# A depthwise convolution's taps, summed in a PSUM bank of their own and cut to the tokens that have an input

## The chip, the cores and the metric

One core of one Trainium2 chip runs the whole program. The metric is the device time of one execution in microseconds (us), lower is better. A kernel's time is the median of its runs.

## The reference, cut to what matters

Three blocks follow one another on 256 tokens of width 1024. The first is two layers of the code below, and the change is in its `_conformer_conv`; of the blocks behind (a recurrent part, an attention with compressed keys, MLPs) the change touches one accumulator only.

```python
for i in range(2):
    h = _rms_norm(x, norm_mix[i])
    q, k, v, cu, cg, ga, gb = split(h @ w_in[i])            # 512 each, ga and gb 1024
    y_a = _dilated_mixture_attention(rope(q), rope(k), v) @ w_attn_out[i]
    y_b = _conformer_conv(cu, cg, ...) @ w_conv_out[i] + b_conv_out[i]
    x = x + (sigmoid(ga) * y_a + sigmoid(gb) * y_b) @ w_out[i]
    x = x + _hier_moe(_rms_norm(x), ...)                    # 32 experts, then a gated projection
...
def _conformer_conv(cu, cg, w_dw, b_dw, ln_g, ln_b):        # 512 channels, 31 taps, causal
    u = cu * jax.nn.sigmoid(cg)
    y = lax.conv_general_dilated(u, rhs, window_strides=(1,), padding=[(CONV_K - 1, 0)], ...)
    return jax.nn.silu(_layer_norm(y + b_dw, ln_g, ln_b))
```

## The kernel before, in words

Activations lie transposed: 128 channels on the partitions, 256 tokens along them. A weight piece is loaded as fp32 (`wload`), cast to a high part on ScalarE (`whi`, L298), and the rest is taken on VectorE (`wlo`, L266); three passes of matmuls over the parts give one product. `ws` sums a strip of 256 output columns in one PSUM tile from the pool `acc` and then calls the strip's sink; `as_` sums two such tiles. `acc` has 4 of the 8 PSUM banks, `aux` the other 4.

A layer (`layer`) goes through: strips of w_in for the gate and the input of the convolution; then strips for q, k and v, with the rotary sinks on VectorE (L559, L560) and GpSimd (L562); attention by pairs of heads; eight strips for ga and gb; the norm of the convolution's result (`norm_silu`); four strips of w_attn_out, each with a sink on VectorE (`sink_a`, L639); four strips of w_conv_out, whose left operand is the normed convolution split in two (`split`, ACT L274 and DVE L275); and w_out. Behind it `moe_ple` streams the experts' weights.

The convolution is done on VectorE, for four groups of 128 channels: one TENSOR_SCALAR for the first tap (L504) and 30 SCALAR_TENSOR_TENSOR (L507), each of which multiplies 256 tokens of `u` (shifted by one) with a weight of each channel and adds what has been summed so far. `u` has 30 zeros in front, so that every tap has 256 tokens. The taps are a generator in the background (`self.bg`): every `wload` pulls four of them (`behind(BG)`), every pair of heads five, and ahead of `norm_silu` the rest is pulled.

`norm_silu` takes the mean over the channels by four matmuls with a matrix of ones (`pm`), subtracts it (L526), squares (ScalarE, L527), sums the squares by eight matmuls of one column each (`pcol`, 16 rows in the trace), forms the reciprocal root (DVE L346, GpSimd L347), spreads it over the tokens by a diagonal matrix (`dg`, L377) and two matmuls (four rows), then multiplies (L539), scales (L540), applies tanh (ScalarE, L542) and the product (L543), and splits (L274, L275).

The order of the instructions on each engine is made before the run: a scheduler takes the program's operations and places them by a simulated timeline (`schedule_with_timeline_sim=True`), under the pools' limits. Each engine then executes its own list strictly in order. SP issues the weight loads; big tiles for activations and for expert pieces come from one pool of slots named `mw`, so an expert piece can be fetched ahead only once a slot is free. In the trace every tile of that pool has the name mw: `u`, the sums, the gates and the expert pieces alike.

Of the kernel before, what the change touches and what calls it, by code (L numbers as in the profile page):

```python
# [16 lines left out]
ALU = mybir.AluOpType  # L17
AX = mybir.AxisListType
PSUM = bass.MemoryType.PSUM
# [3 lines left out]
T = 256  # L23
# [6 lines left out]
CK = 31  # L30
# [15 lines left out]
NACC = 4  # L46
# [172 lines left out]
class Kern:  # L219
    def __init__(self, ctx, tc, a, out):  # L220
        self.tc, self.nc, self.a, self.out, self.ctx = tc, tc.nc, a, out, ctx
        self.uid = 0
        self.bg = iter(())
        ec = ctx.enter_context
        self.cp = ec(tc.tile_pool(name="cp", bufs=1))
        self.wp = ec(tc.tile_pool(name="wp", bufs=WP))
        self.wq = ec(tc.tile_pool(name="wq", bufs=WQ))
        self.sm = ec(tc.tile_pool(name="sm", bufs=2))
        self.acc = ec(tc.tile_pool(name="acc", bufs=NACC, space=PSUM))
        self.aux = ec(tc.tile_pool(name="aux", bufs=8 - NACC, space=PSUM))  # L230
        self.hp = ec(tc.tile_pool(name="hp", bufs=3))
        self.loads, self.gates = [], ()
        self.dr = ec(tc.tile_pool(name="dr", bufs=1, space=DRAM))
# [3 lines left out]
        return f"{s}_{self.uid}"  # L237

    def ps(self, pool=None):
        return (pool or self.acc).tile([P, 512], F32, tag="ps", name=self.n("ps"))  # L240

    def h8(self, dt=F32):
# [41 lines left out]
    def wload(self, key, nk, p0=0):  # L284

        nc = self.nc
        raw = self.wp.tile([P, 1024], F32, tag="raw", name=self.n("raw"))
        o, kp, n = BL[key]
        ps = slice(p0, p0 + kp)
        self.loads.append(nc.sync.dma_start(raw[ps, :n], self.block(key)))  # L290
        if len(self.loads) in self.gates:
            with self.tc.issue_after(self.loads[-1].ins):
                i = len(self.ahead)
                self.ahead.append(self.epiece(self.mr, "mw", *self.first_piece(i)))
        hi = self.wq.tile([P, 1024], F32R, tag="whi", name=self.n("whi"))
        lo = self.wq.tile([P, 1024], F32R, tag="wlo", name=self.n("wlo"))
        hv, lv = hi[ps, :n], lo[ps, :n]
        nc.scalar.copy(hv, raw[ps, :n])  # L298
        self.sub(lv, raw[ps, :n], hv)
        self.behind(BG)  # L300
        r = "p (k n) -> p k n"
        return hv.rearrange(r, k=nk), lv.rearrange(r, k=nk)
# [155 lines left out]
    def layer(self, l):  # L458
        nc, tc, a = self.nc, self.tc, self.a
        vec = self.vec  # L460
        self.l = l
        w_in = ("w_in", l)
        act = self.act_h
        if l == 0:
# [9 lines left out]
        with tc.tile_pool(name=f"d1_{l}", bufs=1) as dp:  # L474

            s8 = self.slot
            r4 = lambda t, o=0: t[:, o:o + 4 * T].rearrange("p (c t) -> p c t", c=4)
            r8 = lambda t: t[:, :8 * T].rearrange("p (c t) -> p c t", c=8)
            u = s8()[:, :4 * (T + CK - 1)].rearrange("p (c t) -> p c t", c=4)
            nc.gpsimd.memset(u[:, :, :CK - 1], 0.0)  # L480

            dB = s8()
            thc = r4(dB)
            quarter = lambda i: dB[:, i * 512:(i + 1) * 512].rearrange("p (c t) -> p c t", c=2)
            vcs = s8()
            cacc = r4(vcs)
            v = vcs[:, 4 * T:8 * T].rearrange("p (t n) -> p t n", t=2)
            w0, bd = VEC["w_dw", l], VEC["b_dw", l]
# [7 lines left out]

            def sink_cu(c, ps):
                c = 2 * (c - 6)
                nc.vector.tensor_tensor(u[:, c:c + 2, CK - 1:], thc[:, c:c + 2, :], ps, op=ALU.mult)

            def conv(cs):
                for c in cs:
                    wc = w0 + c * CK
                    nc.vector.tensor_scalar(cacc[:, c, :], u[:, c, 0:T], vec[:, wc:wc + 1], vec[:, bd + c:bd + c + 1], op0=ALU.mult, op1=ALU.add)  # L504
                    yield
                    for j in range(1, CK):
                        nc.vector.scalar_tensor_tensor(cacc[:, c, :], u[:, c, j:j + T], vec[:, wc + j:wc + j + 1], cacc[:, c, :],  # L507
                                                       op0=ALU.mult, op1=ALU.add)
                        yield
            for i in range(2):  # L510
                self.ws(w_in, 2048 + 256 * i, 256, P, act, sink_cg)
                if l == 0 and i == 1:
                    with tc.issue_after(self.loads[5].ins):
                        nc.sync.dma_start(self.cst[:, 2 * P:], a["consts"][:, 2 * P:])
                        nc.sync.dma_start(self.rv, a["rv"])
                        nc.sync.dma_start(self.nv, a["nv"])
                self.ws(w_in, 1536 + 256 * i, 256, P, act, sink_cu)
                self.bg = itertools.chain(self.bg, conv((2 * i, 2 * i + 1)))
# [392 lines left out]

    def moe_ple(self, l):
        nc, tc, a = self.nc, self.tc, self.a
        self.npiece, self.gates, self.ny = 0, (), 0
        with tc.tile_pool(name=f"m1_{l}", bufs=1) as mp:
            posm, posr, gE, gates = self.route(l, mp)
            pp = self.slot().rearrange("p (t d) -> p t d", t=2)
# [180 lines left out]
    def block2(self):  # L1098
        nc, tc, a, cp = self.nc, self.tc, self.a, self.cp
        vec = self.vec  # L1100
# [18 lines left out]
        with tc.tile_pool(name="rn", bufs=1) as rp, tc.tile_pool(name="rn2", bufs=2) as r2:  # L1119
# [43 lines left out]
            for b in range(4):  # L1163
# [6 lines left out]
                for o in range(3):  # L1170
                    c = 3 * b + o
# [51 lines left out]
        with tc.tile_pool(name="ns1", bufs=1) as sp_, tc.tile_pool(name="ns2", bufs=2) as s2p, tc.tile_pool(name="ns3", bufs=4) as s3p:  # L1223
            s8 = lambda dt=F32: sp_.tile([P, 2080], dt, tag="s8", bufs=4, name=self.n("s8"))
# [41 lines left out]
            nc.gpsimd.memset(hid, 0.0)  # L1266
            w2 = sp_.tile([P, 2, 2, HD], F32, name="w2")
            hs_ = sp_.tile([P, 256], F32, name="hs")
            php = self.ps()
            nz = NG * NC_  # L1270
            phi = ("phi_k", "phi_v")
            for kv, nm in enumerate(phi):
# [19 lines left out]
            for i in range(2):  # L1292
# [9 lines left out]
                for c in range(4 * i, 4 * i + 4, 2):  # L1302
                    ps = self.ps(self.aux)
# [4 lines left out]
            for i in range(2):  # L1308
# [10 lines left out]
                ps = self.ps(self.aux)  # L1319
# [2 lines left out]
                        nc.tensor.transpose(ps[:, gp * T + tt * P:gp * T + (tt + 1) * P], kn[:, tt, gp * P:(gp + 1) * P], self.ident)  # L1322
                nc.scalar.activation(kT[:, 0:2, i, :], ps.rearrange("p (g t) -> p g t", g=2), AF.Copy, scale=nv[:, 1 + i:2 + i])

            pht = self.ps(self.aux)
            for kv in range(2):
                o = 64 * kv
# [15 lines left out]
            ps = self.ps(self.aux)  # L1343
# [12 lines left out]
            ps = self.ps(self.aux)  # L1356
# [4 lines left out]
            ps = self.ps(self.aux)  # L1361
# [10 lines left out]
            for cp_ in range(2):  # L1372
                ps = self.ps(self.aux)
# [5 lines left out]
            for tt in range(2):  # L1379
# [6 lines left out]
                pv = pc[:, tt, :, :, 0:ncb].rearrange("p r g c -> p (r g) c")  # L1386
# [13 lines left out]
            for r in range(4):  # L1400
                ps = self.ps(self.aux)
# [8 lines left out]
            for c in range(8):  # L1410
# [3 lines left out]
                for tt in range(2):  # L1414
                    w = P if tt == 0 else T
# [134 lines left out]
```

## Time and profile before

| | us |
|---|---|
| median of 3 runs | 1913.4 (1908.98 to 1913.78) |
| profiled execution | 1918.83, its span 1916.7 |
| layer 0 / layer 1 in the span | about 0 to 200 / 660 to 865 |
| expert stages | about 210 to 645, and to 1310 |
| last blocks | about 1320 to 1916 |
| busy over the span: TensorE, VectorE, ScalarE, GpSimd | 1634.9, 855.2, 577.8, 61.4 |
| granted TensorE clock, mean | 0.906 of full speed |

The shares of the whole span hide the stages: the two layers use all engines, the two expert stages wait for the memory. The layers, where the change is, have to be read by themselves.

### The profile page before, as it was taken

Reading aid. Unit: us, or ns where it says so; the run is one execution under the profiler, and the core shown is the slowest. Engines: PE = TensorE matmul, PEld = TensorE weight load, DVE = VectorE, ACT = ScalarE, POOL = GpSimd, SP = SyncE. Lnnn points to the kernel's source line nnn. Section 1 sums busy time; section 2 is a strip of 40 time slices with the busy share of each in tenths; the row PEclk is TensorE's granted clock in tenths of the full one; section 3 lists DMA queues with packets and bytes.
Section 4 is the critical chain, followed back from the end, with each engine's and each line's share of the span. In section 5 each row is a group of like instructions: output and inputs, shape, how many; then the busy total and the mean of one; then the engine's idle time right before and its main releaser. Section 6 shows DMA issues by size and latency. Waiting matters only on the chain. (4 is left out here: it accounts for less than half of the span.)

```text
span 1916.7 us, 28139 instructions
## 1 busy us (share of the span) xinstructions
PE 1634.9 (85%) x11355; PEld 1099.3 (57%) x11355; DVE 855.2 (45%) x1760; ACT 577.8 (30%) x1033; POOL 61.4 (3%) x74
## 2 busy tenths in 40 slices
PE   8998887766767999989766576689999999999999
PEld 8898431221213698884311221147897778679987
DVE  8987220111101399862110110015888656556643
ACT  4455110001001445541100000025464444445532
POOL 0100000000000010000000000000011100000000
PEclk9999897787788999999978887899999989789999
DMA  7658899999999675598999999995757633235554
GB/s 284 220 177 302 339 426 427 427 425 426 427 427 426 281 277 165 193 334 356 426 427 427 424 426 426 427 426 205 219 167 237 203 99 104 66 98 186 185 190 134
DMA packets 109725, 567.29 MB, mean 296 GB/s; under 512 B 12106, under 2 KB 21258, under 8 KB 61712
## 3 DMA queue, kind: packets, MB, share of 16 engines
q1 hardware_dynamic: 102976, 558.45, 75.3%
q10 hardware_dynamic: 5984, 5.82, 1.0%
q8 instruction: 94, 1.54, 0.3%
q0 software_dynamic: 624, 1.09, 0.2%
q14 instruction: 47, 0.39, 0.1%
HBM read 561.48 MB, written 3.83 MB: 295 GB/s over the span
## 5 line engine op out<-in xcount | busy, mean ns | idle before, releaser
L261 PE MATMUL ps<-mw,h 128*32 128x512 f32 x2032 | 319.5, 731 | 131.3 <-DMA mw<-in_w_exp_up_dram 70.6
L298 ACT CAST whi<-raw 128x1024 fp32r<-128x1024 f32 (+3 forms) x286 | 294.8, 1034 | 445.2 <-PE ps L261 222.9
L266 DVE TENSOR_TENSOR wlo<-raw,whi 128x1024 fp32r<-128x1024 f32 (+3 forms) x286 | 342.5, 1200 | 183.3 <-ACT whi L298 173.9
L261 PE MATMUL ps<-h,whi 128*128 128x256 f32 x2208 | 293.8, 282 | 4.9 <-ACT h L413 2.4
L261 PEld LDWEIGHTS ps<-h,whi 128*128 128x128 f32 x2208 | 273.3, 188 | 10.3 <-ACT h L413 3.4
L261 PEld LDWEIGHTS ps<-mw,h 128*32 128x32 f32 x2032 | 50.5, 118 | 338.2 <-DMA mw<-in_w_exp_up_dram 164.2
L261 PE MATMUL ps<-mw,mw 128*32 128x512 f32 (+3 forms) x1584 | 144.2, 466 | 39.9 <-DMA mw<-in_w_exp_down_dram 34.2
L261 PE MATMUL ps<-h,wlo 128*128 128x256 f32 x1104 | 154.4, 281 | 0.5 <-DVE wlo L266 0.5
L261 PEld LDWEIGHTS ps<-h,wlo 128*128 128x128 f32 x1104 | 140.4, 188 | 1.3 <-DVE wlo L266 0.7
L910 DVE TENSOR_TENSOR x<-x,ps 128x512 f32<-128x512 f32 (+2 forms) x60 | 34.6, 581 | 217.2 <-PE ps L261 217.2
L845 ACT ACTIVATE mw<-ps 128x512 f32<-128x512 f32 x16 | 9.5, 596 | 401.1 <-PE ps L261 401.1
L846 DVE TENSOR_TENSOR mw<-mw,ps 128x512 f32<-128x512 f32 x16 | 11.0, 687 | 266.7 <-issue 141.9
L261 PEld LDWEIGHTS ps<-mw,mw 128*32 128x32 f32 (+1 forms) x1584 | 47.3, 115 | 123.6 <-DMA mw<-in_w_exp_down_dram 69.2
L507 DVE SCALAR_TENSOR_TENSOR mw<-mw,vec,mw 128x256 f32<-128x256 f32 x240 | 111.3, 510 | 0.0
L261 PEld LDWEIGHTS ps<-h,h 128*128 128x128 f32 x512 | 68.0, 205 | 63.7 <-issue 55.2
L818 DVE TENSOR_TENSOR h<-ps,vec 128x256 f32<-128x256 f32 (+1 forms) x80 | 29.7, 371 | 167.3 <-PE ps L261 167.2
L261 PE MATMUL ps<-whi,h 128*128 128x512 f32 (+1 forms) x512 | 104.2, 345 | 0.0
L261 PE MATMUL ps<-mw 128*128 128x512 f32 (+4 forms) x328 | 91.1, 447 | 14.4 <-ACT mw L904 14.2
L261 PE MATMUL ps<-h,h 128*128 128x128 f32 x512 | 78.2, 299 | 16.0 <-issue 10.5
L261 PEld LDWEIGHTS ps<-whi,h 128*128 128x128 f32 x512 | 79.0, 190 | 16.3 <-issue 3.8
L261 PEld LDWEIGHTS ps<-mw 128*128 128x128 f32 (+1 forms) x328 | 45.4, 196 | 60.2 <-ACT mw L904 35.8
L904 ACT COPY mw<-ps 128x512 f32<-128x512 f32 (+2 forms) x50 | 21.6, 432 | 193.1 <-PE ps L261 193.1
(340 smaller groups left out, 1850.7 us busy)
## 6 DMA issues: line engine op xcount, KB each, us to landing
mw<-in_w_exp_gate_dram SPq DMA_DIRECT2D x128, 1024.0 KB, 19.6
mw<-in_w_exp_up_dram SPq DMA_DIRECT2D x126, 1024.0 KB, 19.6
mw<-in_w_exp_down_dram SPq DMA_DIRECT2D x118, 1024.0 KB, 19.6
raw<-in_w_in_dram SPq DMA_DIRECT2D x129, 512.0 KB, 4.5
raw<-in_w_mlp_in_dram SPq DMA_DIRECT2D x32, 512.0 KB, 3.5
raw<-in_w_mlp_out_dram SPq DMA_DIRECT2D x32, 512.0 KB, 3.5
raw<-in_w_out_dram SPq DMA_DIRECT2D x24, 512.0 KB, 4.4
raw<-in_w_ple_gate_dram SPq DMA_DIRECT2D x16, 512.0 KB, 16.8
```

Source lines behind the costliest of these rows:

```text
L261: return self.nc.tensor.matmul(out, lhsT, rhs, start=start, stop=stop)
L266: self.nc.vector.tensor_tensor(lo, src, hi.bitcast(F32), op=ALU.subtract)
L298: nc.scalar.copy(hv, raw[ps, :n])
L507: nc.vector.scalar_tensor_tensor(cacc[:, c, :], u[:, c, j:j + T], vec[:, wc + j:wc + j + 1], cacc[:, c, :], op0=ALU.mult, op1=ALU.add)
L818: nc.vector.tensor_tensor(xg[:, k:k + n, :], ps[:, :n * P].rearrange("p (k s) -> p k s", k=n), self.vec[:, gcol + k:gcol + k + n].unsqueez ...
L845: nc.scalar.activation(sg, G, AF.Silu)
L846: nc.vector.tensor_tensor(sg, sg, U, op=ALU.mult)
L904: nc.scalar.copy(ys[i], Y[:, :dw])
L910: nc.vector.tensor_tensor(xs, xs, pc[:, :dw], op=ALU.add)
```

## The change

The pool `acc` gets three banks, and a new pool `one` gets the fourth. Outside the layers every fourth accumulator comes from `one`, as if nothing had changed; inside a layer (`apart`) `one` belongs to the convolution and the strips go round on three. The convolution's running sum lies in a tile of `one`, two channel groups in one tile, and the last tap writes the result to SBUF. `u` loses its 30 zeros: tap d works on tokens d to 255 alone, 256 - d of them, in the order d = 0, 30, 29, ... 1; since the tap d = 1 writes tokens 1 to 255 only, a copy on ScalarE carries token 0 of each group over. One accumulator (`php`) of a later block also comes from `one`.

```diff
@@ -226,7 +226,10 @@
         self.wp = ec(tc.tile_pool(name="wp", bufs=WP))
         self.wq = ec(tc.tile_pool(name="wq", bufs=WQ))
         self.sm = ec(tc.tile_pool(name="sm", bufs=2))
-        self.acc = ec(tc.tile_pool(name="acc", bufs=NACC, space=PSUM))
+        self.acc = ec(tc.tile_pool(name="acc", bufs=NACC - 1, space=PSUM))
+
+        self.one = ec(tc.tile_pool(name="one", bufs=1, space=PSUM))
+        self.apart, self.nps = False, 0
         self.aux = ec(tc.tile_pool(name="aux", bufs=8 - NACC, space=PSUM))
         self.hp = ec(tc.tile_pool(name="hp", bufs=3))
         self.loads, self.gates = [], ()
@@ -237,6 +240,10 @@
         return f"{s}_{self.uid}"
 
     def ps(self, pool=None):
+        if pool is None and not self.apart:
+            self.nps += 1
+            if self.nps % NACC == 0:
+                pool = self.one
         return (pool or self.acc).tile([P, 512], F32, tag="ps", name=self.n("ps"))
 
     def h8(self, dt=F32):
@@ -458,7 +465,7 @@
     def layer(self, l):
         nc, tc, a = self.nc, self.tc, self.a
         vec = self.vec
-        self.l = l
+        self.l, self.apart = l, True
         w_in = ("w_in", l)
         act = self.act_h
         if l == 0:
@@ -476,13 +483,12 @@
             s8 = self.slot
             r4 = lambda t, o=0: t[:, o:o + 4 * T].rearrange("p (c t) -> p c t", c=4)
             r8 = lambda t: t[:, :8 * T].rearrange("p (c t) -> p c t", c=8)
-            u = s8()[:, :4 * (T + CK - 1)].rearrange("p (c t) -> p c t", c=4)
-            nc.gpsimd.memset(u[:, :, :CK - 1], 0.0)
+            u = r4(self.held())
 
             dB = s8()
             thc = r4(dB)
             quarter = lambda i: dB[:, i * 512:(i + 1) * 512].rearrange("p (c t) -> p c t", c=2)
-            vcs = s8()
+            vcs = self.held()
             cacc = r4(vcs)
             v = vcs[:, 4 * T:8 * T].rearrange("p (t n) -> p t n", t=2)
             w0, bd = VEC["w_dw", l], VEC["b_dw", l]
@@ -496,17 +502,21 @@
 
             def sink_cu(c, ps):
                 c = 2 * (c - 6)
-                nc.vector.tensor_tensor(u[:, c:c + 2, CK - 1:], thc[:, c:c + 2, :], ps, op=ALU.mult)
+                nc.vector.tensor_tensor(u[:, c:c + 2, :], thc[:, c:c + 2, :], ps, op=ALU.mult)
+
 
             def conv(cs):
+                pv = self.ps(self.one).rearrange("p (c t) -> p c t", c=2)
                 for c in cs:
-                    wc = w0 + c * CK
-                    nc.vector.tensor_scalar(cacc[:, c, :], u[:, c, 0:T], vec[:, wc:wc + 1], vec[:, bd + c:bd + c + 1], op0=ALU.mult, op1=ALU.add)
+                    w = lambda d: vec[:, w0 + c * CK + CK - 1 - d:w0 + c * CK + CK - d]
+                    ac = pv[:, c % 2]
+                    nc.vector.tensor_scalar(ac, u[:, c, :], w(0), vec[:, bd + c:bd + c + 1], op0=ALU.mult, op1=ALU.add)
                     yield
-                    for j in range(1, CK):
-                        nc.vector.scalar_tensor_tensor(cacc[:, c, :], u[:, c, j:j + T], vec[:, wc + j:wc + j + 1], cacc[:, c, :],
-                                                       op0=ALU.mult, op1=ALU.add)
+                    for d in range(CK - 1, 0, -1):
+                        dst = cacc[:, c, :] if d == 1 else ac
+                        nc.vector.scalar_tensor_tensor(dst[:, d:], u[:, c, :T - d], w(d), ac[:, d:], op0=ALU.mult, op1=ALU.add)
                         yield
+                    nc.scalar.copy(cacc[:, c, 0:1], ac[:, 0:1])
             for i in range(2):
                 self.ws(w_in, 2048 + 256 * i, 256, P, act, sink_cg)
                 if l == 0 and i == 1:
@@ -911,7 +921,7 @@
 
     def moe_ple(self, l):
         nc, tc, a = self.nc, self.tc, self.a
-        self.npiece, self.gates, self.ny = 0, (), 0
+        self.npiece, self.gates, self.ny, self.apart = 0, (), 0, False
         with tc.tile_pool(name=f"m1_{l}", bufs=1) as mp:
             posm, posr, gE, gates = self.route(l, mp)
             pp = self.slot().rearrange("p (t d) -> p t d", t=2)
@@ -1266,7 +1276,8 @@
             nc.gpsimd.memset(hid, 0.0)
             w2 = sp_.tile([P, 2, 2, HD], F32, name="w2")
             hs_ = sp_.tile([P, 256], F32, name="hs")
-            php = self.ps()
+            self.apart = True
+            php = self.ps(self.one)
             nz = NG * NC_
             phi = ("phi_k", "phi_v")
             for kv, nm in enumerate(phi):
@@ -1322,6 +1333,7 @@
                         nc.tensor.transpose(ps[:, gp * T + tt * P:gp * T + (tt + 1) * P], kn[:, tt, gp * P:(gp + 1) * P], self.ident)
                 nc.scalar.activation(kT[:, 0:2, i, :], ps.rearrange("p (g t) -> p g t", g=2), AF.Copy, scale=nv[:, 1 + i:2 + i])
 
+            self.apart = False
             pht = self.ps(self.aux)
             for kv in range(2):
                 o = 64 * kv
```

How the change moves instructions shows on two engines. First VectorE, layer 0, around the sinks of attn_out (L639 before, L649 now). `mw_844` and `mw_852` are the gate that a sink updates, `wlo` a weight's low part, `mw_168` before and `ps_832` now the running sum, L526 and L536 the first step of `norm_silu` behind the taps. Before:

```order
L626 TENSOR_TENSOR mw_846<-ps_1568,rB_154 128x512
L266 TENSOR_TENSOR wlo_1699<-raw_1696,whi_1698 128x1024
L507 SCALAR_TENSOR_TENSOR mw_168<-mw_165,vec,mw_168 128x256 x3
L275 TENSOR_TENSOR mw_841<-ps_1019,mw_841 128x256
L507 SCALAR_TENSOR_TENSOR mw_168<-mw_165,vec,mw_168 128x256 x5
L639 SCALAR_TENSOR_TENSOR mw_844<-mw_844,ps_1631 128x512
L266 TENSOR_TENSOR wlo_1731<-raw_1728,whi_1730 128x1024
L526 TENSOR_TENSOR mw_168<-mw_168,ps_1449 128x256 x4
L639 SCALAR_TENSOR_TENSOR mw_844<-mw_844,ps_1663 128x512
L266 TENSOR_TENSOR wlo_1763<-raw_1760,whi_1762 128x1024
L639 SCALAR_TENSOR_TENSOR mw_844<-mw_844,ps_1695 128x512
```

Now, the sinks of the third and the fourth strip and what follows (the widths go on from 239 to 251 between this piece and the next):

```order
L649 SCALAR_TENSOR_TENSOR mw_852<-mw_852,ps_1705 128x512
L517 SCALAR_TENSOR_TENSOR ps_832<-mw_168,vec,ps_832 128x234
L273 TENSOR_TENSOR wlo_1810<-raw_1807,whi_1809 128x1024
L517 SCALAR_TENSOR_TENSOR ps_832<-mw_168,vec,ps_832 128x235
L649 SCALAR_TENSOR_TENSOR mw_852<-mw_852,ps_1737 128x512
L517 SCALAR_TENSOR_TENSOR ps_832<-mw_168,vec,ps_832 128x236
L273 TENSOR_TENSOR wlo_1847<-raw_1844,whi_1846 128x1024
L517 SCALAR_TENSOR_TENSOR ps_832<-mw_168,vec,ps_832 128x237
L517 SCALAR_TENSOR_TENSOR ps_832<-mw_168,vec,ps_832 128x238
```
```order
L517 SCALAR_TENSOR_TENSOR ps_832<-mw_168,vec,ps_832 128x252
L517 SCALAR_TENSOR_TENSOR ps_832<-mw_168,vec,ps_832 128x253
L517 SCALAR_TENSOR_TENSOR ps_832<-mw_168,vec,ps_832 128x254
L517 SCALAR_TENSOR_TENSOR mw_171<-mw_168,vec,ps_832 128x255
L536 TENSOR_TENSOR mw_171<-mw_171,ps_1459 128x256 x4
```

Before, the last tap stands ahead of the first sink of attn_out. Now 20 taps of the last channel group (widths 236 to 255) stand behind the sink of the fourth strip; in layer 1 it is 18.

Second TensorE, the same place: strips of attn_out (`mw_841` or `mw_849` on the left), the matmuls of the norm (`ones`, `cst`, `dg`), and the first of conv_out (`mw_842` or `mw_850`). Before:

```order
L261 MATMUL ps_1727<-mw_841,whi_1730 128x256 x12
L261 MATMUL ps_1462<-cst,mw_167 128x1
L261 MATMUL ps_1727<-mw_841,whi_1730 128x256
L261 MATMUL ps_1462<-cst,mw_167 128x1
L261 MATMUL ps_1727<-mw_841,whi_1730 128x256 x3
L261 MATMUL ps_1727<-mw_841,wlo_1731 128x256 x6
L261 MATMUL ps_1462<-cst,mw_167 128x1
L261 MATMUL ps_1727<-mw_841,wlo_1731 128x256
L261 MATMUL ps_1462<-cst,mw_167 128x1 x5
L261 MATMUL ps_1727<-mw_841,wlo_1731 128x256
L261 MATMUL ps_1476<-dg_1475,cst 128x128 x2
L261 MATMUL ps_1759<-mw_842,whi_1762 128x256
```

Now:

```order
L268 MATMUL ps_1705<-mw_849,whi_1708 128x256 x16
L268 MATMUL ps_1705<-mw_849,wlo_1709 128x256 x8
L268 MATMUL ps_1737<-mw_849,whi_1740 128x256 x16
L268 MATMUL ps_1737<-mw_849,wlo_1741 128x256 x8
L268 MATMUL ps_1459<-mw_171,ones_92 128x256
L268 MATMUL ps_1472<-cst,mw_170 128x1 x8
L268 MATMUL ps_1486<-dg_1485,cst 128x128 x2
L268 MATMUL ps_1769<-mw_850,whi_1772 128x256
```

Before, the norm's matmuls are mixed into the strips of attn_out. Now they stand behind its last strip, and there is nothing else for TensorE between that strip and conv_out.

Further ahead a count is enough: on VectorE 39 taps stand ahead of the low part of the first piece of v's weights in layer 0 before and 25 now, in layer 1 41 before and 26 now.

## Rows read from the trace of the kernel before

**Rows 1.** The page: chain of work that ended last, by engine.
```profile
PE 27%; DVE 2%; DMA 1%; ACT 1%; issue 0%; DVEq 0%; ACTq 0%
```

**Rows 2.** Stretches: length, busy PE, PEld, DVE, ACT, POOL; clock, DMA share, GB/s.
```profile
48.00:96.00 48.00, 45.33 (x312) 39.92 (x312) 48.00 (x101) 22.59 (x42) 8.21 (x11) 0.96 0.62 219
...
150.00:160.00 10.00, 4.17 (x28) 3.81 (x28) 7.58 (x22) 3.40 (x9) 0.72 (x1) 0.74 0.80 251
200.00:210.00 10.00, 6.98 (x33) 4.16 (x32) 5.94 (x37) 2.32 (x7) 0.49 (x1) 0.52 0.45 174
300.00:400.00 100.00, 72.24 (x390) 16.94 (x388) 9.22 (x18) 4.12 (x7) 0.00 (x0) 0.76 1.01 427
```

**Rows 3.** Timeline of TensorE: start, duration, what; idle before and releaser.
```profile
65.53 1.58 PE L261 MATMUL ps<-wlo,h 128*128 128x512 f32 x4 [2.55 <-DVE wlo L266]
...
725.00 1.20 PE L261 MATMUL ps<-wlo,h 128*128 128x512 f32 x4 [0.99 <-DVE wlo L266]
...
729.24 1.20 PE L261 MATMUL ps<-wlo,h 128*128 128x512 f32 x4 [1.17 <-DVE wlo L266]
```

**Rows 4.** Timeline of TensorE, layer 0, end of attn_out to conv_out.
```profile
143.46 0.59 PE L261 MATMUL ps<-mw,ones 128*128 128x256 f32 x2
...
150.52 1.17 PE L261 MATMUL ps<-cst,mw 128*128 128x1 f32 x10
151.55 0.36 PE L261 MATMUL ps<-mw,wlo 128*128 128x256 f32 x1
154.12 0.68 PE L261 MATMUL ps<-dg,cst 128*128 128x128 f32 x4 [2.21 <-DVE dg L377]
158.43 5.38 PE L261 MATMUL ps<-mw,whi 128*128 128x256 f32 x31 [3.63 <-ACT mw L274]
```

**Rows 5.** Timeline of TensorE, layer 1, the same place.
```profile
811.15 0.60 PE L261 MATMUL ps<-dg,cst 128*128 128x128 f32 x4
816.65 5.45 PE L261 MATMUL ps<-mw,whi 128*128 128x256 f32 x31 [4.89 <-ACT mw L274]
```

**Rows 6.** Timeline of VectorE, layer 0: last taps, first sink, wlo, subtractions.
```profile
139.08 2.06 DVE L507 SCALAR_TENSOR_TENSOR mw<-mw,vec,mw 128x256 f32<-128x256 f32 x5
143.42 0.69 DVE L639 SCALAR_TENSOR_TENSOR mw<-mw,ps 128x512 f32<-128x512 f32 x1 [2.28 <-PE ps L261]
144.03 1.22 DVE L266 TENSOR_TENSOR wlo<-raw,whi 128x1024 fp32r<-128x1024 f32 x1
145.16 1.41 DVE L526 TENSOR_TENSOR mw<-mw,ps 128x256 f32<-128x256 f32 x4
```

**Rows 7.** Timeline of VectorE, layer 1: root, diagonal, first multiplication.
```profile
809.26 0.15 DVE L346 TENSOR_SCALAR ms<-ps 128x2 f32<-128x2 f32 x1
810.25 0.48 DVE L377 TENSOR_SCALAR dg<-cst,rc 128x128 f32<-128x128 f32 x2 [0.83 <-POOL rc L347]
...
813.09 1.41 DVE L539 TENSOR_TENSOR mw<-mw,ps 128x256 f32<-128x256 f32 x4
```

**Rows 8.** Groups by line and form: busy us, mean ns of one; idle before.
```profile
L507 DVE SCALAR_TENSOR_TENSOR mw<-mw,vec,mw 128x256 f32<-128x256 f32 x240 | 111.3, 510 | 0.0
L414 DVE SCALAR_TENSOR_TENSOR h<-ps,vec,h 128x256 fp32r<-128x256 f32 x32 | 14.2, 480 | 1.4 <-ACT h L413 0.8 <-PE ps L261 0.5
L910 DVE TENSOR_TENSOR x<-x,ps 128x256 f32<-128x256 f32 x12 | 5.1, 422 | 45.0 <-PE ps L261 44.9
L527 ACT ACTIVATE mw<-mw 128x256 f32<-128x256 f32 x8 | 2.9, 408 | 0.0
```

**Rows 9.** Line 507 by itself: min/median/max ns, first and last start.
```profile
L507 DVE SCALAR_TENSOR_TENSOR mw<-mw,vec,mw x240: 448/479/971, 29.1 to 798.5; 128x256 f32<-128x256 f32 x120
```

**Rows 10.** Timelines of VectorE and GpSimd, layer 0, rotary sinks.
```profile
53.84 2.22 DVE L507 SCALAR_TENSOR_TENSOR mw<-mw,vec,mw 128x256 f32<-128x256 f32 x3
...
52.87 1.65 POOL L562 TENSOR_TENSOR mw<-mw 128x256 f32<-128x256 f32 x1 [3.86 <-DVE mw L560]
```

**Rows 11.** Timeline of SyncE's queue: first expert piece issued behind the taps.
```profile
141.17 0.33 SPq L800 DMA_DIRECT2D mw<-in_w_exp_up_dram  x1
```

## The prediction

> **What bounds the kernel now.** I read the chain that ended last first: TensorE holds by far the largest share of it, 27%, VectorE 2% [rows 1]. So a change on VectorE counts only where TensorE waits for it. Next come the stretches. In the q and k strips of layer 0 VectorE is busy for all of 48 us, while TensorE works 45.33 of them [rows 2]: both are near full. Between attn_out and conv_out it is the other way: in the 10 us from 150 on TensorE is busy for 4.17, at a granted clock of 0.74. The expert stage behind the layer is bound by memory: 427 GB/s and DMA engines full from 300 to 400. But at 200 to 210, where it begins, they are busy for 0.45 only, so this stage begins when the layer lets it and a later layer moves it whole.
>
> Then the waits of TensorE in the layers. It waits for a weight's low part, which stands behind taps on VectorE, 2.55 us once in layer 0 and 0.99 and 1.17 us in layer 1 [rows 3]. And it waits for the norm of the convolution: attn_out's last matmul ends at 151.55 + 0.36 = 151.91, conv_out begins at 158.43 [rows 4]; in layer 1 the ends are 811.15 and 816.65 [rows 5]. The last taps of layer 0 end at 139.08 + 2.06 = 141.14, ahead of attn_out's first sink at 143.42 [rows 6]; so the mean, the squares and the sums run under attn_out, and only the last part of the norm is seen.
>
> **What a tap costs.** Five taps in a row take 2.06 us [rows 6]; with the median of 0.479 us for one [rows 9] they start (2.06 - 0.48) / 4 = 0.395 us apart. What a token costs: VectorE needs 422 ns for 256 columns with a PSUM operand [rows 8] and 0.69 us for 512 [rows 6], so (690 - 422) / 256 = 1.04 ns. The mean tap loses 15.5 tokens, 16 ns, and 120 taps of a layer 1.9 us. The taps of the tail, 237 to 255 tokens, lose 10 ns: 0.39 us each.
>
> What a tap costs with its sum in PSUM no row shows, since no VectorE row writes there. Reading is shown: the same operation with one input in PSUM and a scalar per partition takes 480 ns [rows 8], against the taps' median of 479; a plain sum with one PSUM input takes 422. I take no change, as the 480 row is the same operation. Below lies 422 (-0.06 us), above the taps that met GpSimd's rotary work: three in 2.22 us [rows 10], 0.74 each, +0.35. That upper row is two engines on SBUF, which a sum in PSUM should ease rather than add, so I hold the far end for unlikely.
>
> [...]
>
> **The change, part by part.** The order of the instructions decides, and it moves. (1) Fewer taps ahead of the first wlo of v: in layer 0 25 instead of 39 stand there, in layer 1 26 instead of 41; 14 x 0.395 = 5.5 us is more than the 2.55 us and the 0.99 + 1.17 us that TensorE waited [rows 3]. I let these waits go: -2.55 and -2.16 us.
>
> (2) The norm's matmuls leave the strips of attn_out. The 16 column matmuls cost 1.17 / 10 = 0.117 us each [rows 4], 1.87 us; one of the mean's goes too, and two of its rows stand 143.46 to 143.70, 0.24 us. With (1), attn_out ends at 151.91 - 2.55 - 1.87 - 0.24 = 147.25 in layer 0 and at 811.15 - 2.16 - 1.87 - 0.24 = 806.88 in layer 1. Three accumulators in place of four cost nothing by this: a sink takes 0.69 us on VectorE [rows 6], a strip has 24 matmuls between two sinks, and its bank is wanted again only two strips later.
>
> (3) The tail. Behind attn_out's last matmul VectorE does that strip's sink (0.6 us to the next start, 143.42 to 144.03), a tap (0.4), a wlo (1.13, 144.03 to 145.16 [rows 6]) and 19 taps at 0.39, 7.4 us; with 0.1 for the handover 9.6 us in layer 0, and with 17 taps 8.85 in layer 1. All of this was done before attn_out ended; now TensorE has nothing else to do and stands.
>
> (4) The chain behind the last tap, which in part was hidden and now is seen whole: ScalarE's copy of token 0, 0 to 0.41 us (the longer by the 408 ns of a whole row of 256 [rows 8]), I take 0.3; one mean matmul 0.59 [rows 4], four subtractions 1.41 [rows 6], the last square 0.41 [rows 8], the column matmuls 1.17 [rows 4] (ten of the sixteen rows, as before: those that stand behind the last square), from the root to the end of the diagonal's matmuls 809.26 to 811.15 + 0.60, 2.49 us [rows 5, 7], and from the first multiplication to conv_out 813.09 to 816.65, 3.56 us [rows 5, 7]. That is 9.93, and with 0.4 for handovers 10.3 us. TensorE comes to it from a pause; the clock in such a stretch was 0.74 in the mean [rows 2], and I add 1.17 us, the column matmuls at half speed (0 to 1.2).
>
> (5) Sum. Conv_out begins at 147.25 + 9.6 + 10.3 + 1.2 = 168.4 in place of 158.43, +10.0 us, and in layer 1 at 806.9 + 8.85 + 10.3 + 1.2 = 827.2 in place of 816.65, +10.6 us: together +20.6. Nothing behind takes it back: the expert stage starts with the layer, and the first expert piece behind the taps is issued at 141.17, right after the last tap freed its slot [rows 11], so fetching ahead starts some 15 us later too; that piece is not needed before 200. The accumulator of the later block I cost at nothing: a block with TensorE as its bound has it under matmuls, and a strip that had to wait for the bank's sink would lose the 0.69 us of one. The zeros of `u` that go and the clears that come lie on GpSimd, busy 8.21 of 48 us [rows 2]; without that cover they would cost a wait of under 1 us.
>
> The profiled execution took 1918.83 us, 5.4 more than the median of 1913.4; the sum gives 1939 for a profile and **1934 us** for the median.
>
> **The rivals.** A is the sum. Without the clock's 2.3 us, with taps of 0.06 us less (38 x 0.06 = 2.3) it is 1929; with TensorE's waits of (1) left as they are (+4.7) and taps 0.1 us dearer (+3.8), 1942.
>
> B: a tap with its sum in PSUM is much dearer. The tail pays at once, 3.8 us for each 0.1 us. The other 104 taps of a layer have cover: VectorE has 20 taps less to do ahead of attn_out's end, 8 us, and 1.9 us by the shorter ones, so 0.1 us on each is free; above it each 0.1 us delays attn_out by 10 us a layer, since VectorE is full there [rows 2]. At +0.2 us: 7.6 + 20.8 more than A, about 1962; at +0.13 about 1945. Against it stands the 480 row.
>
> C: the expert stage takes the delay up, because pieces fetched ahead cover its beginning; then 1913 to 1924, by how much of the 20.6 us is absorbed. For it speaks that the DMA engines are not full at 200 to 210, so that a burst could be caught up; against it that the slots are full by then and the stage itself runs at 427 GB/s, which leaves no room.
>
> D, faster: taps are relieved. Their mean is 510 against a median of 479 ns [rows 8, 9], and three beside GpSimd's work took 2.22 us [rows 10]; with one operand less in SBUF this goes, 240 x 31 ns = 7.4 us of VectorE, the waits of (1) go with it, and 1913.4 - 4.7 = 1909 would be left if the tail were hidden. It decides only if the tail and the norm's chain fit between 147.25 and 158.43, in 11.2 us. The chain alone takes 10.3, so the order would have to let the 20 taps run earlier, and it puts them behind the sink; D then needs TensorE to gain over 8 us a layer before attn_out, where it was idle for 2.67 us of 48 [rows 2].
>
> **How the numbers follow.** A 0.62, B 0.16, C 0.11, D 0.11. A alone spans 1929 to 1942. The range 1916 to 1952 leaves out D (0.11), half of C (0.05) and the end of B (0.04). What a measurement of this kernel can tell from no change is about 0.3%, 5.7 us. Faster: most of D and a little of C, 0.10. Same: the rest of D and a part of C, 0.08. Slower: 0.82.
>
> **What would show it.** Right: in layer 0 TensorE ends attn_out near 147, VectorE works through 20 taps at 0.39 us without a gap, conv_out starts near 168, and near 837 in layer 1; the waits before the first v strip are gone; the expert stages are as long as before. Wrong: taps in PSUM 0.1 us or more off 0.39; conv_out at 160 or before; expert stages shorter by what the layers lost.

## The result, and the profile after

The change made the kernel slower: 1937.43 us median of 6 runs (1924.74 to 1944.34) against 1910.77 of 6 (1906.62 to 1913.78), ratio 1.0133, 95% interval 1.0107 to 1.016. The forecast was 1934, and the layers behave as case A had it, but for the spacing of the taps. The profiled execution has a span of 1933.6 us.

The order put 20 taps behind attn_out's last sink; the timeline of VectorE in layer 0 of the changed kernel shows them (against [rows 6]):

```profile
145.27 0.46 DVE L517 SCALAR_TENSOR_TENSOR ps<-mw,vec,ps 128x236 f32<-128x236 f32 x1
145.64 1.22 DVE L273 TENSOR_TENSOR wlo<-raw,whi 128x1024 fp32r<-128x1024 f32 x1
146.78 9.20 DVE L517 SCALAR_TENSOR_TENSOR ps<-mw,vec,ps 128x237 f32<-128x237 f32 x18
156.02 0.48 DVE L517 SCALAR_TENSOR_TENSOR mw<-mw,vec,ps 128x255 f32<-128x255 f32 x1
158.00 1.42 DVE L536 TENSOR_TENSOR mw<-mw,ps 128x256 f32<-128x256 f32 x4 [1.50 <-PE ps L268]
```

The last tap ends at 156.50, before it was 141.14. Between the first of the eighteen and the last tap lie 156.02 - 146.78 = 9.24 us: 0.513 us a tap, not 0.39. Over the whole layer the widths in the trace run from 226 to 255 four times over, so one channel group is finished before the next begins. TensorE, the same place (against [rows 4]):

```profile
143.53 1.10 PE L268 MATMUL ps<-mw,wlo 128*128 128x256 f32 x8
156.74 1.22 PE L268 MATMUL ps<-mw,ones 128*128 128x256 f32 x2 [12.11 <-ACT mw L519]
158.98 3.58 PE L268 MATMUL ps<-cst,mw 128*128 128x1 f32 x16 [1.02 <-ACT mw L537]
163.93 1.22 PE L268 MATMUL ps<-dg,cst 128*128 128x128 f32 x4 [1.37 <-DVE dg L384]
168.91 5.32 PE L268 MATMUL ps<-mw,whi 128*128 128x256 f32 x31 [3.76 <-ACT mw L281]
```

Attn_out ends at 144.63, 7.3 us earlier than before, and then TensorE stands for 12.11 us and goes through the norm's chain alone: 24.3 us to conv_out, where there were 6.5. The wait is put down to ScalarE's copy of token 0 (L519), but the copy itself stood behind the last tap and took 0.16 us from 156.53. Layer 1, TensorE (against [rows 5]):

```profile
817.58 1.10 PE L268 MATMUL ps<-mw,wlo 128*128 128x256 f32 x8
829.79 1.22 PE L268 MATMUL ps<-mw,ones 128*128 128x256 f32 x2 [11.11 <-ACT mw L519]
...
841.89 3.35 PE L268 MATMUL ps<-mw,whi 128*128 128x256 f32 x14 [3.69 <-ACT mw L281]
```

The stretches of [rows 2], now:

```profile
150.00:160.00 10.00, 2.24 (x7) 1.52 (x7) 7.48 (x17) 1.52 (x5) 0.00 (x0) 0.50 0.32 108
...
48.00:96.00 48.00, 48.00 (x347) 42.58 (x347) 43.98 (x86) 26.05 (x49) 8.10 (x6) 1.00 0.62 209
300.00:400.00 100.00, 70.63 (x408) 18.68 (x412) 8.91 (x19) 3.54 (x6) 0.00 (x0) 0.80 1.01 427
```

From 150 to 160 TensorE works 2.24 us, at a granted clock of 0.50, after it stood for 12.11 us. In the q and k strips it is now busy for all 48 us and VectorE is relieved, 43.98: the change does give what a reader of the diff would hope for, but ahead of the place where it loses more. The expert stage is as it was, 427 GB/s from 300 to 400.

To see where the time goes, these are marks of the profiles: the first conv_out sink of layer 0 (a), the first gate sink of layer 1 (b), the first conv_out sink of layer 1 (c), the last sum of the second expert stage (d), and the rest of the span behind it (e). Each kernel has one profile, before and after have two (the second are runs r1 and r2 below).

| kernel | a | b | c | d | e |
|---|---|---|---|---|---|
| before | 166.1 | 681.6 | 824.4 | 1318.6 | 598.1 |
| before, again | 166.5 | 682.4 | 825.3 | 1322.1 | 586.0 |
| after | 176.5 | 693.9 | 850.7 | 1345.5 | 588.1 |
| after, again | 177.4 | 693.6 | 850.1 | 1345.2 | 593.8 |
| e1, sum in SBUF | 164.9 | 683.2 | 823.9 | 1320.4 | 595.3 |
| e2, two banks | 162.8 | 684.9 | 822.4 | 1317.4 | 597.8 |
| e3, three accumulators | 166.8 | 682.9 | 825.8 | 1324.8 | 580.3 |
| e5b, one chain in SBUF | 175.2 | 697.0 | 851.4 | 1351.5 | 592.7 |
| e6, two banks in layers | 162.3 | 683.2 | 825.2 | 1323.6 | 587.7 |
| e10, one of two in PSUM | 166.0 | 681.9 | 822.5 | 1316.8 | 591.7 |
| e7, cut taps alone | 163.5 | 678.8 | 821.6 | 1315.8 | 582.8 |
| e8, one strip behind | 162.0 | 679.8 | 818.0 | 1314.9 | 587.3 |
| e9, two strips behind | 160.5 | 677.3 | 816.5 | 1312.1 | 577.1 |

At d the change has cost 26.9 and 23.1 us in the two pairs, 25 in the mean, of the 26.7 between the medians. The rest, e, differs by 12 us between two executions of the same program before, and by 6 after.

### The profile page after: what moved, and what is told of

The parts are those of the page before. It is cut to its first block, busy times and chain, and to the rows that moved or that the text cites. A ratio compares the mean times of both kernels' runs of the same rounds, so it can differ in the third digit from the quotient of the medians.

```text
span 1933.6 us, 28167 instructions
## 1 busy us (share of the span) xinstructions
PE 1632.8 (84%) x11355; PEld 1097.6 (57%) x11355; DVE 862.9 (45%) x1760; ACT 579.0 (30%) x1041; POOL 60.0 (3%) x76
## 5 line engine op out<-in xcount | busy, mean ns | idle before, releaser
L268 PE MATMUL ps<-h,wlo 128*128 128x256 f32 (+1 forms) x1104 | 152.9, 280 | 0.0
L268 PEld LDWEIGHTS ps<-h,wlo 128*128 128x128 f32 (+1 forms) x1104 | 139.8, 189 | 0.0
L517 DVE SCALAR_TENSOR_TENSOR ps<-mw,vec,ps 128x226 f32<-128x226 f32 (+28 forms) x232 | 108.7, 469 | 3.8
L828 DVE TENSOR_TENSOR h<-ps,vec 128x256 f32<-128x256 f32 (+1 forms) x80 | 29.7, 371 | 165.1 <-PE ps L268 164.9
```

Of the source, the lines that this page charges most:

```text
L268: return self.nc.tensor.matmul(out, lhsT, rhs, start=start, stop=stop)
L517: nc.vector.scalar_tensor_tensor(dst[:, d:], u[:, c, :T - d], w(d), ac[:, d:], op0=ALU.mult, op1=ALU.add)
L828: nc.vector.tensor_tensor(xg[:, k:k + n, :], ps[:, :n * P].rearrange("p (k s) -> p k s", k=n), self.vec[:, gcol + k:gcol + k + n].unsqueez ...
```

## The experiments

Theory T: the time is the taps that stand behind attn_out and the norm's chain that they uncover; they stand there because the channel groups' chains no longer alternate. Rivals: the three accumulators or the cut taps (A3), and the price of a sum in PSUM (P).

Each ratio below is to the kernel before as it ran beside that experiment: a median of 1912.55 us for e1, e2, e3 and e5, 1914.57 for e5b, e6, e7 and e10, 1910.07 for e8 and e9. It is estimated from all these runs and differs from the quotient of the medians by up to 0.002.

**e1_sbuf_sum**, the sum back in SBUF, all else as changed:

```diff
-                pv = self.ps(self.one).rearrange("p (c t) -> p c t", c=2)
-                    ac = pv[:, c % 2]
+                    ac = cacc[:, c, :]
...
-                        dst = cacc[:, c, :] if d == 1 else ac
-                        nc.vector.scalar_tensor_tensor(dst[:, d:], ...
+                        nc.vector.scalar_tensor_tensor(ac[:, d:], ...
-                    nc.scalar.copy(cacc[:, c, 0:1], ac[:, 0:1])
```

> The changed kernel with the running sum in SBUF as before; the taps are cut to the tokens that have an input, and the strips keep three accumulators. Two channel groups' chains alternate again and all 120 taps and the norm's subtractions stand ahead of attn_out's sinks. Theory T (the time is the 20 and 18 taps behind attn_out and the norm's chain that they uncover): 1905 to 1913 us, no change against before or slightly faster, conv_out's first matmul in layer 0 by 158 us. Rival A3 (three accumulators, or the cut taps, cost it): 1925 or more, with attn_out's strips waiting.

Measured 1910.66 us, ratio to before 0.9982 (0.9961 to 1.0003). In its order all taps stand ahead of attn_out's sinks, widths of two groups in turn. The loss is gone with three accumulators and cut taps in place: A3 falls for both.

**e3_three_acc**, three accumulators alone, put into the kernel before (with the changed kernel's rules for which accumulator comes from `one`):

```diff
-        self.acc = ec(tc.tile_pool(name="acc", bufs=NACC, space=PSUM))
+        self.acc = ec(tc.tile_pool(name="acc", bufs=NACC - 1, space=PSUM))
+        self.one = ec(tc.tile_pool(name="one", bufs=1, space=PSUM))
...
```

> The kernel before with three accumulators for the strips of the layers and nothing else (one bank idle there). Theory T: 1906 to 1916 us, no change. Rival A3: most of the 26.7 us, 1925 or more.

Measured 1908.15 us, 0.9975 (0.9956 to 0.9994). A3 falls a second time. Its last blocks were short in its profile (580.3), its d was not.

**e2_two_banks**, the sum in PSUM, but each group of a pair in a bank of its own:

```diff
-        self.one = ec(tc.tile_pool(name="one", bufs=1, space=PSUM))
+        self.one = ec(tc.tile_pool(name="one", bufs=2, space=PSUM))
-        self.aux = ec(tc.tile_pool(name="aux", bufs=8 - NACC, space=PSUM))
+        self.aux = ec(tc.tile_pool(name="aux", bufs=7 - NACC, space=PSUM))
...
-                    ac = pv[:, c % 2]
+                    ac = self.ps(self.one)[:, :T]
```

> The changed kernel with two PSUM banks for the sums, one for each channel group, and three in place of four banks for the attention. The chains of two groups alternate, 117 of 120 taps stand ahead of attn_out's sinks. Theory T: 1908 to 1918 us (a little for the attention's lost bank). Rival P (a tap with its sum in PSUM is 0.12 us dearer, that is the cost): the taps start 0.51 us apart also here, 240 x 0.12 = 29 us of VectorE, of which some 10 us a layer are covered: 1920 or more. T with the rest of the 0.51 being the wait of a tap for the one before it: alternating taps start 0.37 to 0.40 us apart.

Measured 1917.2 us, 1.0019 (1.0004 to 1.0034). That is within T's 1908 to 1918, and nearly all of the loss is gone. Its VectorE timeline has four taps of two groups in turn (widths 235, 236, 236, 237), and what starts next:

```profile
105.38 1.58 DVE L516 SCALAR_TENSOR_TENSOR ps<-mw,vec,ps 128x235 f32<-128x235 f32 x4
106.91 1.23 DVE L273 TENSOR_TENSOR wlo<-raw,whi 128x1024 fp32r<-128x1024 f32 x1
```

1.53 us for four, 0.38 each, with the sums in PSUM. So 0.51 is not the price of PSUM, and rival P falls.

**e5_sbuf_serial**, a single chain in SBUF:

```diff
...
-                    nc.vector.tensor_scalar(ac, u[:, c, :], w(0), vec[:, bd + c:bd + c + 1], ...
+                    nc.vector.tensor_scalar(ac, u[:, c, :], w(0), cacc[:, c - 1, T - 1:T] if c else vec[:, bd + c:bd + c + 1], ...
...
```

> The sum in SBUF with cut taps, but each channel group's chain made to wait for the one before it: its first tap adds the last token of the group before in place of the bias, which changes the result. The order puts 15 taps (layer 0) and 13 (layer 1) behind attn_out's fourth sink. Theory T: slower than before by what the tail and the norm's chain cost, 1926 us (1922 to 1931): the changed kernel less five taps of 0.5 us a layer and 0.12 us on each of the others. Rival P: 1905 to 1913, since no sum is in PSUM. The distance of two taps of one chain shows by the way whether 0.51 us is the price of PSUM (then 0.39 here) or of a chain (then 0.51 here).

Measured 2675.61 us. The other values send tokens to other experts, and the expert stages did different work (3440 matmuls more), so nothing behind layer 0 compares; the expectation had missed that. Layer 0 is still read: 14 taps of the tail lay in 7.13 us, (7.13 - 0.48) / 13 = 0.51 us apart in SBUF too, and the first conv_out sink came at 172.8.

**e5b_sbuf_chain**, the same without a change of values:

```diff
...
+                    b = vec[:, bd + c:bd + c + 1]
+                    if c:
+                        bb = self.sm.tile([P, 1], F32, tag="bb", name=self.n("bb"))
+                        nc.vector.tensor_scalar(bb, cacc[:, c - 1, T - 1:T], 0.0, b, op0=ALU.mult, op1=ALU.add)
+                        b = bb
...
```

> Sum in SBUF, cut taps, three accumulators, and each channel group's chain made to wait for the one before: a small VectorE instruction (one column) takes the last token of the group before times zero plus the bias and hands that as the bias. The result is that of the reference. 17 taps (layer 0) and 15 (layer 1) stand behind attn_out's fourth sink, against 20 and 18 in the changed kernel. Theory T (the order of a serial chain, and nothing of PSUM, is the cost): 1929 to 1936 us, conv_out's first matmul in layer 0 near 166, taps of the tail 0.51 us apart. Rival P (the sum in PSUM costs it): 1905 to 1916.

Measured 1951.44 us, 1.0202 (1.0169 to 1.0236): the loss is back, and larger, with no sum in PSUM. VectorE and then TensorE, layer 0:

```profile
147.06 8.15 DVE L520 SCALAR_TENSOR_TENSOR mw<-mw,vec,mw 128x240 f32<-128x240 f32 x16
156.52 1.42 DVE L538 TENSOR_TENSOR mw<-mw,ps 128x256 f32<-128x256 f32 x4 [1.31 <-PE ps L268]
```
```profile
155.26 1.22 PE L268 MATMUL ps<-mw,ones 128*128 128x256 f32 x2 [10.36 <-DVE mw L520]
...
167.36 5.58 PE L268 MATMUL ps<-mw,whi 128*128 128x256 f32 x31 [3.69 <-ACT mw L281]
```

(8.15 - 0.48) / 15 = 0.511 us a tap. The place and the mechanism are as T says (conv_out at 167.36, expected near 166); the size is missed by 15 us or more. The layers do not hold that: a and c - b are below those of the changed kernel, 8.9 and 11.5 us above the kernel before, 20.4 together where the change made it 24.5. From a to b it takes 521.8 us against 517.4 and 516.2, from c to d 500.1 against 494.8 and 495.1. Why its expert stages are 5 us longer stays open.

**e10_one_of_two**, the changed kernel with every second group's sum in SBUF:

```diff
-                    ac = pv[:, c % 2]
+                    ac = cacc[:, c, :] if c % 2 else pv[:, 0]
...
```

> The changed kernel with the even channel groups summed in the one PSUM bank and the odd ones in SBUF, so that two chains alternate with one bank. 114 and 117 of 120 taps stand ahead of attn_out's sinks. Theory T: 1902 to 1914 us, the tail is gone. Rival P: half of the sums in PSUM, half of the loss: 1920 to 1927.

Measured 1912.11 us, 0.9984 (0.9966 to 1.0002). One bank, half of the taps still on a sum in PSUM, and the tail is gone; VectorE at the end of the taps:

```profile
144.73 0.47 DVE L517 SCALAR_TENSOR_TENSOR mw<-mw,vec,ps 128x255 f32<-128x255 f32 x1
145.32 0.69 DVE L650 SCALAR_TENSOR_TENSOR mw<-mw,ps 128x512 f32<-128x512 f32 x1
```

The last tap stands ahead of the fourth sink. TensorE, the same place:

```profile
144.22 1.07 PE L268 MATMUL ps<-mw,wlo 128*128 128x256 f32 x8
145.57 1.13 PE L268 MATMUL ps<-mw,ones 128*128 128x256 f32 x4 [0.29 <-ACT mw L520]
...
157.39 5.77 PE L268 MATMUL ps<-mw,whi 128*128 128x256 f32 x26 [3.69 <-ACT mw L281]
```

Attn_out ends at 145.29 and conv_out starts 12.1 us later, so the norm's chain is nearly as bare here as in the changed kernel. What differs is the tail: the last tap ends 11.3 us earlier (145.20 against 156.50) and conv_out starts 11.5 us earlier (157.39 against 168.91). The uncovered chain alone costs the layer nothing against before (158.43), since attn_out ends 6.6 us earlier; the tail is the loss. Of the edits tried this is the smallest that undoes it.

**e6_two_in_layers**, two banks in the layers, given back outside them:

```diff
...
+        elif pool is self.aux and self.apart is not True:
+            self.nax += 1
+            if self.nax % (8 - NACC) == 0:
+                pool = self.two
...
+                    ac = self.ps((self.one, self.two)[c % 2])[:, :T]
```

> Sums in two PSUM banks inside the layers as in the run with two banks, but outside the layers the attention's fourth bank is given back, so that the expert stages have four. Theory T: the layers gain 3 us and 5 us as that run's profile shows, the expert stages take as long as before: 1900 to 1907 us, faster than both kernels. Rival: the 6 us that the expert stage was longer in that run are not the lost bank, but the layer's gain given back (the stream ends when it ends): 1909 to 1918.

Measured 1910.92 us, 0.9982 (0.9965 to 1.0). A miss, within the range of its rival: layer 0 gains its 4 us (a), but from a to b it takes 520.9 us in place of 515.5, with the attention's fourth bank back. The lost bank was not what made e2's expert stage longer.

**e7_cut_taps**, the cut taps alone, four accumulators and sums in SBUF:

```diff
-            u = s8()[:, :4 * (T + CK - 1)].rearrange("p (c t) -> p c t", c=4)
-            nc.gpsimd.memset(u[:, :, :CK - 1], 0.0)
+            u = r4(self.held())
...
+                    for d in range(CK - 1, 0, -1):
+                        nc.vector.scalar_tensor_tensor(ac[:, d:], u[:, c, :T - d], w(d), ac[:, d:], op0=ALU.mult, op1=ALU.add)
```

> The kernel before with the taps cut to the tokens that have an input and nothing else: sum in SBUF, four accumulators. Theory T: 1903 to 1912 us, no change or a little faster (4 us of VectorE less in two layers, of which TensorE sees little). Rival (the cut taps themselves cost it, by their unaligned starts or their lengths): 1920 or more.

Measured 1901.46 us, 0.9925 (0.9902 to 0.9948): faster than both kernels, and by more than was expected. 3 us of it are there at a, 3 to 6 at d; the rest lies in the last blocks, whose code is the same and whose instructions the scheduler ordered anew. Whether that order is worth something is not settled, since one program alone varies by 12 us there.

**r1_before_again and r2_after_again**, both kernels unchanged.

> The kernel before, unchanged, for a second profile. If the last blocks take the same time for the same order of instructions: 598 us from the end of the second expert stage to the end, as in the first profile. If they vary from execution to execution by the granted clock (0.74 in one stretch of the first profile): 585 to 595, and the ends of the layers and expert stages within 2 us of the first profile.

> The changed kernel, unchanged, for a second profile. Theory T: end of the second expert stage near 1345 us again, tail taps 0.51 us apart, conv_out's first matmul near 169 and 842. The rest, the last blocks, 585 to 600.

1910.05 and 1940.85 us in one execution each. After: d at 1345.2 and conv_out's first matmul at 168.73 and 841.58, as expected. Before: d at 1322.1, 3.5 us from the first profile, more than the 2 expected; e is 586.0 against 598.1.

**e8_gate_strip_behind and e9_two_strips_behind**: e7 with one or two gate strips written behind attn_out:

```diff
-            for i in range(8):
+            for i in range(7):
                 self.ws(w_in, 2560 + 256 * i, 256, P, act, sink_g)
...
+            self.ws(w_in, 2560 + 256 * 7, 256, P, act, sink_g)
             for i in range(4):
                 self.ws(("w_conv_out", l), 256 * i, ...
```

> Cut taps in SBUF and four accumulators, and the last of the eight gate strips written behind attn_out in place of ahead of it, so that TensorE has 6 us of work between attn_out and conv_out. Theory T (TensorE stands there for the norm alone): the 6.5 and 4.9 us that it waited there in the kernel before go, 1890 to 1897 us. Rival: attention ends no earlier, attn_out waits for it instead, 1899 to 1906.

> The same with the last two gate strips behind attn_out. Theory T: no more to gain than with one, since the wait was 6.5 us, and attn_out may now wait for the attention: 1888 to 1903 us. Rival: 1903 or more, since attention's matmuls stand late on TensorE.

Measured 1900.05 us, 0.9925 (0.9899 to 0.9952), and 1897.05 us, 0.9932 (0.9906 to 0.9958). TensorE's wait at conv_out in layer 0, 4.86 us in e7, shrinks in e8 to

```profile
151.75 1.33 PE L261 MATMUL ps<-mw,whi 128*128 128x256 f32 x9 [0.85 <-ACT mw L274]
...
154.45 5.21 PE L261 MATMUL ps<-mw,whi 128*128 128x256 f32 x29 [1.37 <-ACT mw L274]
```

and in e9 none is left, as T says; but of the wait removed a shows 1.5 and 3 us against e7, and the times are not told apart from e7's. e8's expectation is missed, e9's is met. e8's time lies in the range of its rival, but the rival's reason is not seen: attn_out ends at 144.80, in e7 at 149.83. Why the shorter waits do not show in the time stays open.

## Why the prediction was right, and what it mis-sized

**The order decides.** Right. The taps stand behind attn_out's last sink and TensorE has nothing else; e1, e2 and e10 take the tail away in three ways and the loss goes, e5b puts the tail back without PSUM and the loss returns.

**(1) and (2), attn_out ends earlier.** Right in kind: the waits ahead of v are gone (in layer 0 TensorE is busy for all of 48 to 96, in layer 1 v's first low part is taken up at 735.00 without a wait). In layer 1 the size fits too (818.68, less the 12.3 us by which mark b moved, is 806.4 against 806.88). In layer 0 it was too small, 144.63 in place of 147.25. What the sum left out there is what came behind the wait in the kernel before (its TensorE timeline, and a stretch with the columns of [rows 2]):

```profile
66.92 3.23 PE L261 MATMUL ps<-whi,h 128*128 128x512 f32 x8
69.98 1.10 PE L261 MATMUL ps<-wlo,h 128*128 128x512 f32 x4
70.92 2.03 PE L261 MATMUL ps<-whi,h 128*128 128x512 f32 x8
72.78 1.46 PE L261 MATMUL ps<-h,whi 128*128 128x256 f32 x11
```
```profile
65.50:70.00 4.50, 4.46 (x13) 3.52 (x14) 4.50 (x14) 2.04 (x5) 1.45 (x2) 0.62 0.32 117
```

After it stood for 2.55 us TensorE went on at a granted clock of 0.62 in the mean: twelve matmuls took 4.45 us from 65.53 [rows 3] to 69.98, and the next twelve of the same shapes 2.80, from 69.98 to 72.78, at a clock of 1.00. With the wait these 1.65 us went as well, of the 2.6 that the sum lacked. Of the rest, 0.46 us is a wait for ScalarE at 138.76 that is gone too; what is left was not traced.

The relief that the prediction's D looked for did come for the taps, though no run shows that it moved attn_out: beside GpSimd's products they now take no longer than elsewhere. Line 517 of the changed kernel, and line 515 of e1, where the sum lies in SBUF with the same cut:

```profile
L517 DVE SCALAR_TENSOR_TENSOR ps<-mw,vec,ps x232: 431/469/488, 28.7 to 828.5; 128x226 f32<-128x226 f32 x4, 128x228 f32<-128x228 f32 x4, 128x230 f32<-128x230 f32 x4, 128x232 f32<-128x232 f32 x4
```
```profile
L515 DVE SCALAR_TENSOR_TENSOR mw<-mw,vec,mw x240: 431/464/945, 29.6 to 796.3; 128x226 f32<-128x226 f32 x4, 128x227 f32<-128x227 f32 x4, 128x228 f32<-128x228 f32 x4, 128x229 f32<-128x229 f32 x4
```

The longest is 488 ns with the sum in PSUM, 945 in SBUF and 971 before [rows 9]. In e2, two groups in turn in PSUM, it is 483, and in e5b, one chain in SBUF, 962, so it goes with where the sum lies and not with the order. GpSimd's rotary products of the same stretch, in pairs, lines 572 and 573 (after) and 562 and 563 (before):

```profile
L572 POOL TENSOR_TENSOR mw<-mw x8: 738/742/1654, 43.1 to 734.2; 128x256 f32<-128x256 f32 x8
L573 POOL TENSOR_TENSOR mw<-mw x8: 734/1720/1728, 43.8 to 735.8; 128x256 f32<-128x256 f32 x8
```
```profile
L562 POOL TENSOR_TENSOR mw<-mw x8: 906/1648/2049, 46.4 to 723.9; 128x256 f32<-128x256 f32 x8
L563 POOL TENSOR_TENSOR mw<-mw x8: 904/914/927, 48.0 to 725.5; 128x256 f32<-128x256 f32 x8
```

The median of the first product falls from 1648 to 742 ns and that of the second rises from 914 to 1720; the sixteen take 8.6 + 10.8 = 19.4 us in place of 12.5 + 7.3 = 19.8. A product's time goes with what VectorE does beside it. Beside taps alone it took 0.90 to 0.93 us before (at 54.48 and 59.82) and takes 0.73 to 0.75 now (at 54.75 and 55.45); each product of 1.6 us or more lies beside a weight's low part for about 1 us or longer, in both kernels (at 52.87 before, at 49.34 now). So a tap and a product side by side are both shorter than before, but GpSimd's time as a whole hardly moved. The first product's 739 ns in e2 and 1620 in e5b do not tell the sum's place from what stood beside it.

**(3), the tail.** The term that was mis-sized. The prediction took 0.395 us from five taps in a row and did not ask whether they belonged to one chain. Every tap reads the sum that the tap before it in its chain wrote, and in the traces each waits on VectorE's own semaphore (240 of 240 taps, before and after). With two groups in turn that one is done in time, and taps start 0.38 us apart in PSUM (e2) and 0.395 in SBUF ([rows 6], and three taps in 1.26 us in e1, whose widths show the two groups). In a single chain a tap starts when the one before has ended, 0.48 + 0.03 = 0.51 us, in PSUM (after) and in SBUF (e5, e5b). For 19 and 17 taps that is 2.3 and 2.0 us more than the sum had. The prediction had named this as a sign that it would be wrong, taps 0.1 us or more off 0.39, and there it was: the tail was right in place and number of taps, and wrong in the price of one.

**PSUM's own price.** None is seen, as taken: with the sum in PSUM a tap has a median of 469 ns in the changed kernel and 464 in e2, with the sum in SBUF 464 in e1 and 466 in e5b, and in e10, which has both, 467 with the sum in PSUM and 466 in SBUF.

**(4), the chain.** 156.50 to 168.91 is 12.4 us against 10.3 + 1.2. All sixteen rows of column matmuls stand in it, at a granted clock of 0.50, 3.58 us where 1.17 + 1.17 were counted. ScalarE's copy was priced at 0.3; 156.50 to 156.74 holds the handovers and the copy.

**(5), the sum.** Conv_out's first matmul moves by 168.91 - 158.43 = 10.5 us in layer 0 (10.0 forecast); in layer 1, counted from mark b, by (841.89 - 693.9) - (816.65 - 681.6) = 12.9 (10.6). In layer 0 the shortfall of (1) and (2), -2.6, and the excess of (3) and (4), +2.2 and +0.9, nearly cancel: that the 10.0 came so close to 10.5 was luck. Together 23.4, and 25 at mark d; nothing behind took it back, so C was wrong. B was wrong in its reason, though a tap in the tail did cost 0.12 us more. The nearness of 1934 to 1937.43 is in part luck too: the loss was forecast as 20.6 us and is 26.7, and the kernel before had 1913.4 in the three runs that the forecast started from, 1910.77 in the six of the comparison.

## What to carry to other kernels

A long sum on one engine should be two sums in turn: here a tap that waited for the tap before paid its whole length, 0.51 us, and taps of two sums in turn started 0.38 to 0.40 us apart. Where a scheduler sets the order, see whether it still keeps two chains apart: here two sums in one PSUM tile became one chain, while sums in one SBUF tile went in turn (e1, e7) and so did sums in two banks (e2, e6). Two tiles in one bank were not tried. The end of the one chain then stood behind other work; look in the new order for what has moved behind the last independent work of the bounding engine, and price that whole, at the clock that the engine was granted after it stood still (0.50 here). When the spacing of a repeated instruction is taken from a trace, say first whether neighbours depend on each other.

## What the runs showed that was not expected

The kernel with cut taps alone is 0.75% faster (e7), but with three accumulators beside them 0.18%, not told from nothing (e1). Up to mark d, where the taps are, e7 shows only 3 to 6 us of its gain, so that the shorter taps are the cause is not shown. From mark a to b, the expert stage with what lies around it, the kernels took 515.3 to 522.1 us though its code is one and the same, and layers that ended 3 to 4 us earlier got nothing for it there in e2 and e6 and kept it in e7; later ones were passed on whole. What sets this was not found.
